# Low halves of sixteen weight panels and the decay masks on VectorE in place of GpSimd, in a two-layer streaming encoder on one core

## The chip, the cores and the metric

The kernel runs as one launch on one core of a Trainium2 chip. Its engines are named as in the profile: PE (TensorE, with PEld for its weight loads), DVE (VectorE), ACT (ScalarE), POOL (GpSimd) and SP (SyncE, whose queue starts most DMAs). The metric is the device time of the launch in microseconds (us); lower is better. Each engine takes its instructions in the order in which the program gives them, so an instruction that waits holds all that stand behind it on its engine.

## What is computed

One sequence of 1024 frames of width 1024 goes through two layers and a last RMSNorm. Layer 0 is chunked softmax attention, layer 1 a gated DeltaNet; each is followed by a squared-ReLU MLP. The change lies in layer 1. Cut to what matters there (chunks of 64 frames, 8 heads of width 128):

```
proj = h @ w_in                           # q, k, v, z of 8 heads each, and the gates a, b
qkv = silu(causal_conv(qkv, conv_w))      # 4 taps
gc = cumsum(g, axis=-1)                   # log decay inside a chunk
decay = exp(where(incl, gc[..., :, None] - gc[..., None, :], -inf))
L = where(strict, einsum('bhnid,bhnjd->bhnij', kb, k) * decay, 0.0)
M = L + eye(CHUNK)
sol = triangular_solve(M, rhs, left_side=True, lower=True, unit_diagonal=True)
qk = einsum('bhnid,bhnjd->bhnij', q, k) * decay
# scan over the 16 chunks:
v_new = u_c - w_c @ state
o_c = qd_c @ state + qk_c @ v_new
state = state * gl_c + kd_c^T @ v_new
```

## The kernel before

Every dense product is made from weight panels of 128 output columns, [128, 8, 128]. Matrices are split into a high and a low part, and each product is three matmuls: high by high, high by low, low by high. So a panel needs a `whi`, which ACT makes as a rounded copy of the loaded `wraw`, and a `wlo`, which is `wraw` less `whi`.

The delta layer (`deltanet`, L1673, to the end of `dn_run`) has 34 panels in the list `jobs` of `dn_ahead`: the keys of heads 0 to 7 (numbers 0 to 7), then q0, v0, q1, v1, q2, v2 (8 to 13), z0, q3 (14, 15), v3 and so on, and last two panels of the output projection. For each of the 32 others PE makes two halves of 512 frames, 24 matmuls each, into one of two PSUM banks (`acc`). The generator `weights` inside `dn_ahead` splits panel n in two pieces of 512 columns, high on ACT and low by `low` (L1015) on DVE or POOL. Panel 0 is split at the end of layer 0's MLP, the others inside `dn_run`.

A half that is done is taken out by `dn_evac` (L2076): DVE multiplies the bank into a tile `xp`, which frees the bank; ACT makes the first products of the convolution (`cy`, `cz`), DVE adds two taps, POOL adds `cy` and `cz`, ACT applies SiLU.

Beside these run the parts of the delta rule, each a generator with a priority:

- `dn_loads` (L2017) loads a row of log decays for each head into one of two tiles, `row` and `vT` in turn. The load for head h+2 waits until head h has used its tile.
- `dn_decays` (L2028) adds the causal mask to that tile in two pieces of 512 columns, then ACT makes eight exponentials of it.
- `dn_blocks` multiplies the key products by it, which gives the tile `U` of a head, and sends its diagonal blocks out. Four heads together are loaded back as `fu`.
- `dn_solves` inverts the 32x32 blocks of four heads by forward substitution, all on DVE: 31 steps, a product into `ft` and a sum into `fz`, of 1 to 961 elements per partition. It runs twice, first for heads 0 to 3, then for heads 4 to 7.
- `dn_scans` runs the scan of a head over 16 chunks: three fp32 matmuls a step on PE (`s<-st,WQ`, `s<-vn,kd`, `s<-vn,qk`) with two short DVE operations between them. Even and odd heads are two chains. The first needs the first forward substitution, the heads 4 to 7 need the second.
- `dn_outs` normalises and gates a head's output, `dn_reload` brings it back as the input of the output projection.

What order the engines see is decided while the program is written out. `Clock` holds a planned time for each engine; every instruction of this layer passes through `Engine.timed` (L160, call on L163, so nearly all of them carry the line L163) and adds its planned cost (`cost`, L106) to its engine. After each dense matmul `turn` gives each task a step when its planned time has come and, for priorities of 1 and more, when the planned backlog of DVE and ACT is below a limit. A DVE operation is planned at another cost than one on POOL, so the move of an operation between the two shifts what the planner puts beside what. The profile has the tile names of the program: `wlo<-wraw,whi` is a low part, `row<-row,mask` and `vT<-vT,mask` are the masks, `ft`, `fz` the forward substitution, `acc<-xs,whi` a dense matmul.

Of the kernel before, what the change touches and what calls it, by code (L numbers as in the profile page):

```python
# [207 lines left out]
class Trunk:  # L208
# [1554 lines left out]
    def dn_ahead(self):  # L1763

        H = 8
        self.jobs = jobs = [("k", n) for n in range(H)] + [(c, n) for n in range(3) for c in "qv"]
        for n in range(3, H):
            jobs += [("z", n - 3), ("q", n), ("v", n)]
        jobs += [("z", n) for n in range(5, H)]
        jobs += [("o", m) for m in range(2)]  # L1770
        raw, panel = {}, {}

        def fetch(n):
            if n < len(jobs):
                c, h = jobs[n]
                raw[n] = self.wp.tile([P, KT, P], F32, name=self.nm("wraw"), tag="wraw")
                self.nc.sync.dma_start(
                    raw[n], self.a["w_od"][h] if c == "o" else self.a["w_in"][8 * "qkvz".index(c) + h])

        def weights(n):  # L1780
            hi = self.wp.tile([P, KT, P], F32R, name=self.nm("whi"), tag="whi")
            lo = self.wp.tile([P, KT, P], F32R, name=self.nm("wlo"), tag="wlo")
            panel[n] = hi, lo
            for s in (slice(0, 4), slice(4, 8)):
                self.high(hi[:, s], raw[n][:, s])
                yield
                self.low(lo[:, s], raw[n][:, s], hi[:, s], True)
                yield
                yield
            fetch(n + 2)  # L1790

        def first():

            nc = self.nc
            ab = self.wp.tile([P, KT, P], F32, name=self.nm("wraw"), tag="wraw")
            nc.sync.dma_start(ab[:, :, 0:16], self.a["w_ab"])
            for _ in range(8):
                yield
            fetch(0)
            yield  # L1800
            yield
            self.wab = w = self.wp.tile([P, KT, P], F32R, name=self.nm("whi"), tag="whi")
            nc.gpsimd.memset(w[:, :, 16:32].bitcast(F32), 0.0)
            self.high(w[:, :, 0:16], ab[:, :, 0:16])
            yield
            self.low(w[:, :, 32:48], ab[:, :, 0:16], w[:, :, 0:16], True)
            yield
            fetch(1)
            yield from weights(0)

        self.panel, self.weights = panel, weights
        return first()
# [215 lines left out]
    def dn_decays(self, odd):  # L2028

        nc = self.nc  # L2030
        yield from self.until("rows")
        for h in range(odd, 8, 2):
            yield from self.until("load", h)
            if h < 2:
                yield from self.until("cols")
            d = self.heads.pop(("load", h))
            v = d.rearrange("p (q t) -> p q t", t=P)
            for q in range(2):
                u = v[:, 4 * q : 4 * q + 4]
                nc.gpsimd.tensor_tensor(  # L2040
                    u, u, self.mask.rearrange("p (o t) -> p o t", o=1).broadcast_to([P, 4, P]), ALU.add)
                yield
            for p in range(8):
                nc.scalar.activation(v[:, p], v[:, p], AF.Exp, bias=self.cols[:, 0, h, p : p + 1])
            yield
            for e in range(2):
                r = slice(64 * e, 64 * e + 64)
                nc.sync.dma_start(self.decay[h, r], v[r, :, r])
            yield
            self.heads["de", h] = d  # L2050
            self.mark("de", h)
            yield
# [614 lines left out]
```

## Time and profile before

| | before |
| --- | --- |
| time, median of 3 runs | 2569.77 us (2567.46 to 2570.54) |
| time of the profiled execution | 2571.22 us |
| its span | 2569.4 us |
| granted TensorE clock, mean | 0.988 |
| delta layer in the trace | about 1208 to 1838 us from the span's start |
| instructions | 36712 |

How to read it: a row of the grouped view gives the line, the engine, the operation, output and inputs, the shapes, the count, then the busy time in us with the mean of one in ns, then the idle time of the engine ahead of these instructions and what ended it. A row of the timeline gives the start in us, the duration, the instruction, its count and in brackets the idle time before it with its releaser. A row of the view of stretches gives the stretch, its length, then for PE, PEld, DVE, ACT and POOL busy time and instruction count, then the granted clock, the DMA share and GB/s.

### The profile page before, as it was taken

What the parts mean: (1) busy time and instruction counts of PE and PEld (TensorE: products, weight loads), DVE (VectorE), ACT (ScalarE), POOL (GpSimd) and SP (SyncE); (2) the same over time, 40 slices, a digit from 0 to 9 for tenths busy, and PEclk for the clock granted to TensorE, in tenths of its full rate; (3) what the DMA queues carried; (4) which work ended last, traced back from release to release, by engine and by line L of the source; (5) the groups of instructions that cost most, each with busy time, mean ns of one, the idle gap of its engine ahead of it and who ended that gap; (6) DMA issues with size and microseconds to landing.
All of it is one profiled execution on the core that took longest, in us unless ns stands there. A gap on an engine that the chain in (4) does not pass through costs nothing.

```text
span 2569.4 us, 36712 instructions
## 1 busy us (share of the span) xinstructions
PE 2466.1 (96%) x12638; PEld 2058.0 (80%) x12638; DVE 1901.5 (74%) x3299; ACT 1210.1 (47%) x2269; POOL 1293.5 (50%) x1088
## 2 busy tenths in 40 slices
PE   8999999999999999998888999999899999999997
PEld 6888888787888788886677788888787888787886
DVE  6665656678887788877578976676678788688887
ACT  6666567535555433334673333333335555433333
POOL 2444355514667466565474333332313766466655
PEclk9999999999999999999998999999999999999998
DMA  4222224424555977843343121122323555967752
GB/s 160 69 65 72 72 78 131 145 83 159 206 209 212 349 237 233 263 148 110 117 143 107 54 83 59 60 81 96 122 99 139 205 205 209 334 236 261 244 175 82
DMA packets 193082, 392.43 MB, mean 153 GB/s; under 512 B 54960, under 2 KB 61552, under 8 KB 192896
## 3 DMA queue, kind: packets, MB, share of 16 engines
q1 hardware_dynamic: 176048, 355.46, 41.3%
q10 hardware_dynamic: 16848, 34.63, 3.5%
q8 instruction: 100, 1.64, 0.3%
q14 instruction: 86, 0.70, 0.1%
HBM read 254.06 MB, written 127.57 MB: 149 GB/s over the span
## 4 chain that ended last, share of the span: by engine, by line
PE 60%; DVE 10%; DMA 5%; issue 3%; ACT 1%; POOL 1%; SPq 0%; ACTq 0%; DVEq 0%; POOLq 0%
PE y L1013 23%; PE z L1013 11%; PE acc L163 9%; PE acc L1013 6%; PE tp L163 4%; PE s L163 3%; PE acc L279 2%; PE acc L278 2%; PE acc L277 2%; DVE ft L163 2%; DMA xs<-gt 1%; DMA wraw<-in_w_down_dram 1%; DVE x L1517 1%; DMA wraw<-in_w_up_dram 1%; DVE wlo L1019 1%
## 5 line engine op out<-in xcount | busy, mean ns | idle before, releaser
L163 PE MATMUL acc<-xs,whi 128*128 128x512 f32 x1808 | 631.3, 412 | 10.0 <-DVE xp L163 6.1
L163 PEld LDWEIGHTS acc<-xs,whi 128*128 128x128 f32 x1808 | 333.3, 191 | 59.6 <-DVE xp L163 6.3
L163 PE MATMUL acc<-xs,wlo 128*128 128x512 f32 x896 | 368.4, 411 | 3.8 <-POOL wlo L163 3.8
L1013 PE MATMUL y<-xs,whi 128*128 128x512 f32 x1008 | 311.7, 390 | 5.2 <-DVE x L1517 1.8
L163 POOL TENSOR_TENSOR wlo<-wraw,whi 128x512 fp32r<-128x512 f32 x126 | 167.7, 1331 | 245.0 <-ACT whi L163 195.2
L1028 POOL TENSOR_TENSOR s<-wraw 128x256 f32<-128x256 f32 (+1 forms) x93 | 89.7, 965 | 353.9 <-DVE a L1019 175.1
L1019 DVE TENSOR_TENSOR wlo<-wraw,whi 128x512 fp32r<-128x512 f32 (+1 forms) x182 | 208.6, 1146 | 28.2 <-ACT whi L1022 28.2
L1013 PEld LDWEIGHTS y<-xs,whi 128*128 128x128 f32 x1008 | 188.9, 188 | 47.1 <-DVE x L1517 2.6
L1022 ACT ACTIVATE whi<-wraw 128x512 fp32r<-128x512 f32 (+2 forms) x191 | 146.5, 767 | 126.1 <-PE y L1013 87.3
L1013 PE MATMUL y<-xs,wlo 128*128 128x512 f32 x504 | 196.9, 391 | 7.0 <-DVE wlo L1019 6.8
L1013 PE MATMUL y<-xs,a 128*128 128x512 f32 x732 | 188.2, 392 | 9.1 <-DVE x L1517 9.1
L1022 ACT ACTIVATE a<-s 128x256 fp32r<-128x256 f32 x122 | 63.9, 525 | 282.2 <-PE y L1013 141.6
L163 PEld LDWEIGHTS acc<-xs,wlo 128*128 128x128 f32 x896 | 171.3, 191 | 29.2 <-POOL wlo L163 5.0
L1517 DVE TENSOR_TENSOR x<-y,x 128x512 f32<-128x512 f32 x240 | 165.1, 688 | 35.9 <-PE y L1013 28.8
L1013 PEld LDWEIGHTS y<-xs,a 128*128 128x128 f32 x732 | 135.9, 188 | 43.6 <-DVE x L1517 13.9
L1013 PE MATMUL acc<-xs,whi 128*128 128x512 f32 x528 | 162.8, 390 | 0.0
L1013 PE MATMUL y<-xs,ahi 128*128 128x512 f32 x512 | 158.7, 391 | 0.3 <-ACT nt L1206 0.3
L1095 DVE TENSOR_TENSOR c<-c 128x512 fp32r<-128x512 f32 x112 | 132.8, 1204 | 28.5 <-POOL c L1025 26.1
L163 POOL TENSOR_SCALAR pr<-pr,rs 128x640 f32<-128x640 f32 (+4 forms) x128 | 88.2, 692 | 129.2 <-DVE rs L163 98.1
L1013 PE MATMUL z<-xs,whi 128*128 128x512 f32 x480 | 147.8, 389 | 0.0
L163 POOL TENSOR_TENSOR cy<-cy,cz 128x512 f32<-128x512 f32 x48 | 69.0, 1438 | 147.1 <-DVE cz L163 125.2
L163 DVE CUSTOM_DVE_ANT_0 pr<-sp,bias 128x640 f32<-128x640 f32 (+4 forms) x128 | 83.8, 655 | 63.9 <-PE sp L163 62.9
(344 smaller groups left out, 6273.9 us busy)
## 6 DMA issues: line engine op xcount, KB each, us to landing
xs<-gt SPq DMA_DIRECT2D x256, 256.0 KB, 4.7
gt<-c SPq DMA_DIRECT2D x112, 512.0 KB, 2.9
wraw<-in_w_up_dram SPq DMA_DIRECT2D x64, 512.0 KB, 3.5
wraw<-in_w_down_dram SPq DMA_DIRECT2D x64, 512.0 KB, 4.5
r<-gr SPq DMA_DIRECT2D x88, 256.0 KB, 3.4
wraw<-in_w_in_dram SPq DMA_DIRECT2D x32, 512.0 KB, 3.4
gr<-ssum ACTq DMA_DIRECT2D x62, 256.0 KB, 3.2
wraw<-in_w_qkv_dram SPq DMA_DIRECT2D x30, 512.0 KB, 3.3
```

Source lines behind the costliest of these rows:

```text
L163: return call(*args, **more)
L277: nc.tensor.matmul(ps, hi[:, k], xh, start=(k == 0), stop=False)
L278: nc.tensor.matmul(ps, hi[:, k], xl, start=False, stop=False)
L279: nc.tensor.matmul(ps, lo[:, k], xh, start=False, stop=(k == KT - 1))
L1013: nc.tensor.matmul(ps, w[:, k], x, start=bool(first and f), stop=bool(last and e), skip_group_check=True)
L1019: self.nc.vector.tensor_tensor(lo, src, hi.bitcast(F32), ALU.subtract)
L1022: self.nc.scalar.activation(hi, src, AF.Copy)
L1028: self.nc.gpsimd.tensor_tensor(out, x, y, ALU.add)
L1095: nc.vector.tensor_tensor(t[z][:, HB:].bitcast(F32R), t[z][:, HB:], t[z][:, :HB], ALU.subtract)
L1517: nc.vector.tensor_tensor(x, ps, x, ALU.add)
```

## The change

The low parts of the panels 0 to 15 are made by DVE in place of POOL, two operations of 128x512 a panel. The sixteen mask additions (eight heads, two pieces of 128x512) are made by DVE as well. Nothing else is edited.

```
@@ -1784,7 +1784,7 @@
             for s in (slice(0, 4), slice(4, 8)):
                 self.high(hi[:, s], raw[n][:, s])
                 yield
-                self.low(lo[:, s], raw[n][:, s], hi[:, s], True)
+                self.low(lo[:, s], raw[n][:, s], hi[:, s], n >= 16)
                 yield
                 yield
             fetch(n + 2)
@@ -2037,7 +2037,7 @@
             for q in range(2):
                 u = v[:, 4 * q : 4 * q + 4]
-                nc.gpsimd.tensor_tensor(
+                nc.vector.tensor_tensor(
                     u, u, self.mask.rearrange("p (o t) -> p o t", o=1).broadcast_to([P, 4, P]), ALU.add)
                 yield
             for p in range(8):
```

So 32 low parts and 16 masks leave POOL for DVE. Because the planner prices them there, the order of the whole delta layer changes on every engine, from panel 1 on. Three places show it.

The first is DVE at the first two rows of decays (`row` is that of head 0, `vT` that of head 1; `gcols` ends the gates). Before, behind the copy into `gcols` the evacuations of the keys follow at once:

```order
L163 TENSOR_TENSOR xp_12549<-acc_12490,R_12294 128x512
L163 COPY gcols<-tp_12552 128x256
L163 SCALAR_TENSOR_TENSOR cy_12574<-xp_12549,convw,cy_12574 128x512
L163 SCALAR_TENSOR_TENSOR cz_12575<-xp_12549,convw,cz_12575 128x512
L163 MEMSET xp_12624 128x3
L163 TENSOR_TENSOR xp_12624<-acc_12567,R_12294 128x512
```

In the changed kernel two masks and a low part stand ahead of that work on the same engine:

```order
L163 TENSOR_TENSOR xp_12550<-acc_12490,R_12294 128x512
L163 COPY gcols<-tp_12553 128x256
L163 TENSOR_TENSOR row_12544<-row_12544,mask 128x512 x2
L163 TENSOR_TENSOR wlo_12569<-wraw_12390,whi_12568 128x512
L163 SCALAR_TENSOR_TENSOR cy_12578<-xp_12550,convw,cy_12578 128x512
L163 SCALAR_TENSOR_TENSOR cz_12579<-xp_12550,convw,cz_12579 128x512
L163 TENSOR_TENSOR vT_12562<-vT_12562,mask 128x512
L163 MEMSET xp_12618 128x3
L163 TENSOR_TENSOR xp_12618<-acc_12566,R_12294 128x512
```

The next evacuation of a bank (`xp_12624`, now `xp_12618`) has moved behind three masks and a low part. The masks wait for the loads of `row` and `vT`.

The second place is DVE in the first forward substitution, from its step of 100 elements on. Before, its steps follow each other:

```order
L163 TENSOR_TENSOR ft_13174<-fz_12321,fu_12320 128x100
L163 TENSOR_REDUCE fz_12321<-ft_13174 128x10
L163 TENSOR_TENSOR ft_13174<-fz_12321,fu_12320 128x121
L163 TENSOR_REDUCE fz_12321<-ft_13174 128x11
L163 TENSOR_TENSOR ft_13174<-fz_12321,fu_12320 128x144
L163 TENSOR_REDUCE fz_12321<-ft_13174 128x12
```

In the changed kernel low parts, masks and an evacuation stand between the same steps:

```order
L163 TENSOR_TENSOR ft_13266<-fz_12321,fu_12320 128x100
L163 TENSOR_REDUCE fz_12321<-ft_13266 128x10
L163 TENSOR_TENSOR wlo_13333<-wraw_13129,whi_13332 128x512
L163 TENSOR_TENSOR vT_13322<-vT_13322,mask 128x512
L163 TENSOR_TENSOR U_13356<-tp_13357,row_13169 128x512
L163 TENSOR_TENSOR ft_13266<-fz_12321,fu_12320 128x121
L163 TENSOR_REDUCE fz_12321<-ft_13266 128x11
L163 TENSOR_TENSOR vT_13322<-vT_13322,mask 128x512
L163 MEMSET xp_13387 128x3
L163 TENSOR_TENSOR xp_13387<-acc_13326,R_12294 128x512
L163 TENSOR_TENSOR wlo_13333<-wraw_13129,whi_13332 128x512
L163 TENSOR_TENSOR ft_13266<-fz_12321,fu_12320 128x144
```

Counted over the whole order of DVE: from the first instruction on `fu` (`frt<-fu`) to the end of the first substitution there stand 134 instructions before and 161 now, 12 of the new ones low parts, 4 masks, 4 `qk`, 2 `vb`, 2 `xp`, and few others. From there to the end of the second there are 194 and 190, 4 of these low parts. At the end of the first 22 halves have been evacuated before and 24 now, at the end of the second 32 and 34. Ahead of `frt<-fu` there are 12 in both, and there stand 14 low parts and 12 masks more than before.

The third place is PE near the end of the layer, in the scan of head 7 (`acc_17844` is its last half of a dense panel, `acc_17900` the output projection). From the tenth to the ninth last `s<-st,WQ` before:

```order
L163 MATMUL s_3782_17904<-st_17891,WQ_17613 128x128
L163 MATMUL acc_17844<-xs_11821,whi_17570 128x512 x2
L163 MATMUL acc_17844<-xs_11821,wlo_17571 128x512
L163 MATMUL acc_17844<-xs_11823,whi_17570 128x512
L163 MATMUL s_3783_17916<-vn_12244,kd_17498 128x128
L163 MATMUL s_3782_17904<-vn_12244,qk_12251 128x128
L163 MATMUL acc_17844<-xs_11823,whi_17570 128x512
L163 MATMUL acc_17844<-xs_11823,wlo_17571 128x512
L163 MATMUL acc_17844<-xs_11825,whi_17570 128x512
L163 MATMUL s_3785_17927<-st_17920,WQ_17613 128x128
```

In the changed kernel, from the tenth last to the eighth last:

```order
L163 MATMUL s_3787_17941<-st_17929,WQ_17626 128x128
L163 MATMUL s_3788_17949<-vn_12244,kd_17499 128x128
L163 MATMUL s_3787_17941<-vn_12244,qk_12251 128x128
L163 MATMUL s_3790_17956<-st_17953,WQ_17626 128x128
L163 MATMUL s_3791_17959<-vn_12245,kd_17499 128x128
L163 MATMUL s_3790_17956<-vn_12245,qk_12251 128x128
L163 MATMUL acc_17900<-xs_17837,whi_17738 128x512 x2
L163 MATMUL acc_17900<-xs_17837,wlo_17739 128x512
L163 MATMUL s_3793_17968<-st_17963,WQ_17626 128x128
```

The dense matmuls that lay between the scan's steps have been used up sooner. From the tenth last `s<-st,WQ` on 57 dense matmuls were left before, and 39 are left now.

More of the change, by code (lines that the diff above doesn't have):

```diff
@@ L1786, in weights @@
                 yield
-                self.low(lo[:, s], raw[n][:, s], hi[:, s], True)
+                self.low(lo[:, s], raw[n][:, s], hi[:, s], n >= 16)
                 yield
@@ L2039, in dn_decays @@
                 u = v[:, 4 * q : 4 * q + 4]
-                nc.gpsimd.tensor_tensor(
+                nc.vector.tensor_tensor(
                     u, u, self.mask.rearrange("p (o t) -> p o t", o=1).broadcast_to([P, 4, P]), ALU.add)
```

## The prediction

> **What bounds the kernel now.** The profile's page comes first. PE is busy nearly throughout, so the whole kernel is near PE's work; DVE has more to do than POOL.
>
> ```profile
> PE 2466.1 (96%) x12638; PEld 2058.0 (80%) x12638; DVE 1901.5 (74%) x3299; ACT 1210.1 (47%) x2269; POOL 1293.5 (50%) x1088
> ```
>
> That average says nothing of the layer that is edited, so the next view is that of stretches: the delta layer cut at the start and the end of the first forward substitution (1302 and 1391 us) and at the end of the second (1500).
>
> ```profile
> core 0: us, PE busy (x) PEld busy (x) DVE busy (x) ACT busy (x) POOL busy (x), PEclk, DMA share, GB/s
> 1208.00:1302.00 94.00, 82.92 (x394) 67.54 (x395) 48.70 (x102) 56.83 (x104) 48.96 (x41) 0.98 0.42 123
> 1302.00:1391.00 89.00, 71.51 (x325) 58.87 (x323) 86.08 (x135) 48.57 (x84) 52.27 (x36) 0.89 0.34 103
> 1391.00:1500.00 109.00, 102.24 (x755) 84.97 (x756) 98.05 (x201) 39.07 (x74) 40.47 (x34) 0.97 0.24 73
> 1500.00:1800.00 300.00, 293.08 (x2035) 257.91 (x2034) 198.77 (x511) 115.24 (x252) 97.69 (x73) 0.99 0.24 79
> ```
>
> DVE is half idle in the first stretch (45 us free), full in the second (86.08 of 89), nearly full in the third (98.05 of 109). From 1500 on PE is the bound (293 of 300). So a DVE operation is cheap before 1302, is paid in full from 1302 to 1391, and from 1500 on only PE's work counts. The waits say the same: of PE's waits from 1302 to 1392 the two longest end on DVE.
>
> ```profile
> PE tp L163 <- DVE vb L163: 6.1, 1, 6.1
> PE acc L163 <- DVE xp L163: 6.1, 1, 6.1
> ```
>
> Ahead of 1302 it is a low part from POOL that stops PE longest:
>
> ```profile
> PE acc L163 <- POOL wlo L163: 3.8, 2, 2.2
> ```
>
> **The change part by part.** 48 operations of 128x512 leave POOL: 32 low parts, 16 masks. Their rows there, and below them the same subtraction as DVE makes it elsewhere in this kernel:
>
> ```profile
> L163 POOL TENSOR_TENSOR wlo<-wraw,whi 128x512 fp32r<-128x512 f32 x126 | 167.7, 1331 | 245.0 <-ACT whi L163 195.2 <-DVE ru L300 26.3 <-PE acc L163 13.4
> L163 POOL TENSOR_TENSOR vT<-vT,mask 128x512 f32<-128x512 f32 x8 | 11.6, 1454 | 2.3 <-DMA vT<-grows 2.3
> L163 POOL TENSOR_TENSOR row<-row,mask 128x512 f32<-128x512 f32 x8 | 10.4, 1305 | 20.5 <-issue 8.6 <-DMA row<-grows 8.5 <-DVE ft L163 3.4
> L1019 DVE TENSOR_TENSOR wlo<-wraw,whi 128x512 fp32r<-128x512 f32 x120 | 121.5, 1013 | 5.0 <-ACT whi L1022 5.0
> L1019 DVE TENSOR_TENSOR wlo<-wraw,whi x182: 674/1176/2330, 554.4 to 2524.0; 128x512 fp32r<-128x512 f32 x120, 128x1024 fp32r<-128x1024 f32 x62
> ```
>
> So **the price** of one on DVE lies between 0.67 us (the shortest) and 1.01 us (the mean, beside a busy POOL). I take 0.82, the middle, since POOL keeps the `cy` and `cz` sums there. No row shows a mask on DVE; it has the same shape and two SBUF inputs, so it gets the same price.
>
> **What a removed POOL operation gives back** is in the timelines of DVE and POOL at the start of the substitution:
>
> ```profile
> 1303.88 0.19 DVE L163 SCALAR_TENSOR_TENSOR ru<-ru,frt 128x32 f32<-128x32 f32 x1
> 1304.10 1.32 DVE L163 SCALAR_TENSOR_TENSOR ru<-ru 128x32 f32<-128x32 f32 x1
> 1305.45 1.22 DVE L163 SCALAR_TENSOR_TENSOR ry<-ru,ry 128x32 f32<-128x32 f32 x1
> 1306.70 1.20 DVE L163 TENSOR_TENSOR ru<-ry 128x32 f32<-128x32 f32 x1
> 1307.94 1.19 DVE L163 SCALAR_TENSOR_TENSOR ru<-ru,frt 128x32 f32<-128x32 f32 x1
> ```
>
> ```profile
> 1304.10 1.27 POOL L163 TENSOR_TENSOR wlo<-wraw,whi 128x512 fp32r<-128x512 f32 x1 [1.44 <-DVE ru L163]
> 1305.34 1.29 POOL L163 TENSOR_TENSOR vT<-vT,mask 128x512 f32<-128x512 f32 x1
> 1306.58 1.28 POOL L163 TENSOR_TENSOR cy<-cy,cz 128x512 f32<-128x512 f32 x1
> 1307.82 1.27 POOL L163 TENSOR_TENSOR cz<-cy,cz 128x512 f32<-128x512 f32 x1
> ```
>
> The same DVE operation takes 0.19 us alone and 1.19 beside a POOL operation: each POOL operation here takes 1.0 us from DVE. That is the upper bound of what one gives back; the lower is 0, where DVE sits idle or reads PSUM. The sum of `ft` bounds it in the whole: the same 31 products in the first substitution and, with POOL less busy, in the second.
>
> ```profile
> L163 DVE TENSOR_TENSOR ft<-fz,fu 128x1 f32<-128x1 f32 (+30 forms) x31 | 32.8, 1057 | 0.5
> ```
>
> ```profile
> L163 DVE TENSOR_TENSOR ft<-fz,fu 128x1 f32<-128x1 f32 (+30 forms) x31 | 27.6, 891 | 0.3
> ```
>
> I take half, 0.5 us. The Trainium skill, "SBUF — State Buffer", section "SBUF: two separate sides", says that VectorE with two SBUF inputs and a GpSimd operation that reads SBUF exclude each other over one port pair for a whole instruction, the loser waiting in full. The four rows above agree. By that rule the moved operations, which have two SBUF inputs, are blocked by the sums that stay on POOL, and block them; that speaks against the change and is the third rival.
>
> Now the terms, in order.
>
> (a) Ahead of 1302 (14 low parts, 12 masks more): 26 x 0.82 = 21 us of DVE, into 45 us of idle time. The cover is there. The path through this stretch is load, mask, exponentials, `U`, the next load. A mask pair falls from 2 x 1.3 to 2 x 0.68, over two rounds about -2.5 us, and PE's 3.8 us for low parts go in part. Against it stands the queue: DVE now waits itself where POOL waited for the load.
>
> ```profile
> 1247.33 1.27 POOL L163 TENSOR_TENSOR row<-row,mask 128x512 f32<-128x512 f32 x1 [7.15 <-DMA row<-grows]
> ```
>
> ```profile
> 1241.58 0.69 DVE L163 TENSOR_TENSOR xp<-acc,R 128x512 f32<-128x512 f32 x1 [0.18 <-PE acc L163]
> 1255.04 1.50 DVE L163 SCALAR_TENSOR_TENSOR cy<-xp,convw,cy 128x512 f32<-128x512 f32 x1 [12.77 <-ACT cy L163]
> ```
>
> Behind the first mask pair now stand a low part, `cy`, `cz` and the evacuation that ran at 1241.58; but DVE stood idle for 12.77 us there anyway. I take -2 us, bounds -6 to +8 (second rival). On SP the loads keep their order behind the stores of `U`.
>
> (b) First substitution, 1302 to 1391, DVE full: 16 moved operations x 0.82 = +13.1. The new order puts other work in as well (two `xp`, a `cy`, two `vb`, less one `U`, each of the shape of the `xp` above and so about 0.7; four `qk` at 0.42; three small ones, 0.3 in all): 2.8 + 1.7 + 0.3 = +4.8. In that stretch 11 low parts and 6 masks leave POOL, 17 x 0.5 = -8.5. Sum +9.4.
>
> ```profile
> L163 DVE TENSOR_TENSOR qk<-tp,dc 64x256 f32<-64x256 f32 x12 | 5.0, 420 | 4.3 <-PE tp L163 4.2
> ```
>
> (c) Second substitution: 4 x 0.82 = +3.3, less 4 x 0.5, less the `qk`, `vb`, `st` that have moved ahead (3.6): -2.3. It ends at -2 + 9.4 - 2.3 = +5.1 us.
>
> (d) By then two halves more are evacuated, 48 dense matmuls. In a full stretch three of them take 0.68 us, so 48 are 10.9 us of PE's work, and PE is the bound from here on: -10.9.
>
> ```profile
> 1318.00 0.39 PE L163 MATMUL acc<-xs,wlo 128*128 128x512 f32 x1
> ...
> 1318.68 0.39 PE L163 MATMUL acc<-xs,wlo 128*128 128x512 f32 x1
> ```
>
> (e) The end of the scan. With nothing dense between, a step takes 2.1 us:
>
> ```profile
> 1809.62 0.38 PE L163 MATMUL s<-st,WQ 128*128 128x128 f32 x2
> ...
> 1819.70 0.46 PE L163 MATMUL s<-st,WQ 128*128 128x128 f32 x2 [0.31 <-ACT o L163]
> ...
> 1821.86 0.49 PE L163 MATMUL s<-st,WQ 128*128 128x128 f32 x2 [0.34 <-DVE st L163]
> ...
> 1837.89 0.39 PE L277 MATMUL acc<-xs,whi 128*128 128x512 f32 x1
> ```
>
> From the tenth last `s<-st,WQ` to the output projection's L277 it took 28.3 us with 57 dense matmuls inside; ten bare steps are 21 us. With 39 inside it is 25.4 us if half of those still hide, 28.3 at most, while 18 (4.1 us) have moved ahead of it. So +1.2 to +4.1; I take +3.
>
> Sum: 5.1 - 10.9 + 3 = **-2.8 us**. The profiled execution took 2571.22 us (span 2569.4), 1.5 above the median of 2569.77; taken from the median this gives 2567.0. A measurement of this kernel can tell about 0.2%, 5.1 us, from no change: the forecast is no change, with a lean to faster.
>
> **The rivals.** First, **faster**: POOL's blocking goes nearly whole (1.0 us each, as in the four rows) and the operations cost 0.68. Then (b) is 10.9 + 4.8 - 17 = -1.3 in place of +9.4, the sum -13.5, the time about 2556. For it: the evacuation for which PE waited 6.1 us stood behind sixteen bare steps and now stands among them. Against it: `ft` lost only 5.2 us more in the first substitution than in the second.
>
> Second, **slower**, by the queue on DVE: the mask pair of head 2 waits for its load with `U` of head 1 behind it, and the load of head 3 waits for that `U`. Before, POOL waited there 8.6 us (the "issue" in the row of `row` masks), and nobody else did. If DVE stands for all of that, the load of head 3, its exponentials, `U` and `fu` come up to 8 us later, and (a) is +8: 2577. It decides from about 5 us of waiting on. For it: the order has that `U` between the two masks. Against it: the load of head 3 queued behind that of head 2 before as well.
>
> Third, **slower**, by the ports: each moved operation takes 1.01 us, as DVE's low parts do elsewhere, and nothing comes back since the remaining sums now hit a denser DVE. (b) gains 3 + 8.5: about 2578.5.
>
> **How the numbers follow.** Forecast 0.40 (own range 2564.6 to 2574.9), first rival 0.33, second 0.17, third 0.10. The range takes in the rivals, 2556 and 2578.5, with the bounds of (e) and the runs' own scatter: 2555 to 2581. Faster by over 0.2%: 0.34; within: 0.39; slower: 0.27.
>
> **What would show it.** POOL has 48 operations fewer and DVE 48 more. In the stretch from `frt` to the last `fz` DVE stays full and is 5 to 12 us longer, while PE's busy time in it rises and its wait for `xp` shrinks; `ft` x31 falls below 32.8 us. `fu` lands about when it did. The second substitution ends some 5 us later, with two halves more done. If `frt` starts over 5 us later with DVE waiting for `row<-grows`, the second rival holds; if the low parts on DVE average 1 us or more, the third; if the first substitution takes no longer than 89 us, the first. A new wait of PE for scan steps around 1500 to 1800 would break (d), which takes PE as the bound there.

## The result and the profile after

The changed kernel takes 2596.14 us in the median (2593.6 to 2597.95, 4 runs) where the kernel before, on the same chip, takes 2570.15 us (2567.46 to 2572.34, 4 runs). The ratio is 1.0095, with a 95% interval of 1.0084 to 1.0107: about **26 us slower**. The forecast was 2567.0 and the range ended at 2581, so the prediction was wrong in sign and in size. The profiled execution took 2597.69 us (span 2595.8), with a mean granted clock of 0.983 (0.988 before).

First, where in the program the time was lost. These are the same four stretches of the view of stretches as before, in the changed kernel (length, then busy time of PE, PEld, DVE, ACT, POOL, then granted clock, DMA share, GB/s):

```profile
1208.00:1302.00 94.00, 83.59 (x398) 68.82 (x397) 55.06 (x124) 56.94 (x106) 21.34 (x20) 0.96 0.45 118
1302.00:1391.00 89.00, 82.75 (x379) 68.83 (x378) 79.80 (x153) 47.02 (x84) 29.14 (x20) 0.90 0.38 108
1391.00:1500.00 109.00, 100.25 (x728) 82.83 (x727) 98.64 (x197) 37.02 (x70) 34.19 (x29) 0.95 0.26 74
1500.00:1800.00 300.00, 280.87 (x1886) 243.31 (x1884) 207.98 (x493) 109.34 (x238) 89.83 (x66) 0.96 0.21 67
```

POOL is emptier in all of them, as intended (21.34 for 48.96 in the first). The row that matters is the last: PE, the bound there before with 293.08 of 300 at a clock of 0.99, now has 280.87 at 0.96, with fewer instructions done.

Second, DVE's waits ahead of 1302 (engine and tile, what it waited for, us in total, times, longest), and the masks' own row:

```profile
DVE row L163 <- DMA row<-grows: 16.7, 3, 6.3
DVE vT L163 <- DMA vT<-grows: 6.6, 1, 6.6
```

```profile
L163 DVE TENSOR_TENSOR wlo<-wraw,whi 128x512 fp32r<-128x512 f32 x30 | 22.6, 756 | 3.8 <-ACT whi L163 3.7
L163 DVE TENSOR_TENSOR vT<-vT,mask 128x512 f32<-128x512 f32 x8 | 6.4, 799 | 13.2 <-DMA vT<-grows 13.2
L163 DVE TENSOR_TENSOR row<-row,mask 128x512 f32<-128x512 f32 x8 | 6.2, 784 | 16.7 <-DMA row<-grows 16.7
```

The moved operations are cheap, 0.76 to 0.80 us each. What is dear is the last column: DVE stands 29.9 us in front of masks whose rows have not landed, and all that is queued behind them stands too.

Third, PE's waits from 1509, the end of the second forward substitution, to the end of the layer:

```profile
PE s L163 <- DVE vn L163: 14.0, 18, 2.2
PE s L163 <- DVE ry L163: 4.5, 3, 2.4
PE s L163 <- DVE st L163: 3.2, 2, 2.6
```

PE now stops 21.7 us for single steps of the scan. In the kernel before, from the end of its second substitution on, the three longest such rows come to 10.8 us:

```profile
PE s L163 <- DVE vn L163: 6.9, 7, 2.1
PE s L163 <- DVE rt L163: 2.9, 1, 2.9
PE s L163 <- DVE xp L163: 1.0, 1, 1.0
```

The milestones of all profiled executions, in us from the span's start, from the timelines: `frt<-fu` (start of the first substitution), the start of its last `fz`, the first `s<-st,WQ` (first scan step), the first L277 (end of the layer), and the last less the third. Each row is from one execution, so a difference of 2 us says nothing.

| kernel | frt | last fz | first scan step | L277 | scan |
| --- | --- | --- | --- | --- | --- |
| before | 1302.1 | 1389.0 | 1428.4 | 1837.9 | 409.5 |
| changed | 1312.5 | 1405.2 | 1450.0 | 1865.7 | 415.7 |
| e1_masks | 1309.7 | 1405.0 | 1450.4 | 1864.6 | 414.2 |
| e2_lows | 1304.0 | 1405.2 | 1450.8 | 1854.0 | 403.2 |
| e3_old_order | 1308.4 | 1399.2 | 1438.5 | 1848.7 | 410.2 |
| e4_new_order | 1313.7 | 1406.1 | 1450.0 | 1863.1 | 413.1 |
| e5_fewer | 1303.5 | 1390.0 | 1428.9 | 1827.6 | 398.7 |
| e6_late | 1309.6 | 1400.5 | 1443.0 | 1852.0 | 409.0 |
| e7_lows_old | 1299.0 | 1383.5 | 1423.2 | 1833.7 | 410.5 |
| e8_front | 1299.2 | 1385.6 | 1424.5 | 1835.7 | 411.2 |
| e9_more | 1307.8 | 1400.4 | 1444.7 | 1863.2 | 418.5 |
| e10_solve5 | 1298.4 | 1382.7 | 1427.0 | 1842.3 | 415.3 |
| e11_solve7 | 1297.7 | 1383.4 | 1424.5 | 1841.7 | 417.2 |
| e12_masks_old | 1303.9 | 1395.4 | 1433.3 | 1841.2 | 407.9 |

The layer is 629.6 us long before (from 1208.3, the start of the gates) and 655.9 after (from 1209.8): the loss lies in it. The scan starts 21.6 us later, and then takes 6.2 us longer than it did, though 97 dense matmuls fewer are left for it (from the first scan step to L277 PE starts 963 before and 866 now). Two questions follow: what makes the scan start later, and why it isn't shorter.

### The profile page after: what moved, and what is told of

It reads as the page before. It is cut to its first block, busy times and chain, and to the rows that moved or that the text cites. A ratio compares the mean times of both kernels' runs of the same rounds, so it can differ in the third digit from the quotient of the medians.

```text
span 2595.8 us, 36691 instructions
## 1 busy us (share of the span) xinstructions
PE 2487.7 (96%) x12638; PEld 2070.3 (80%) x12638; DVE 1931.1 (74%) x3347; ACT 1206.4 (46%) x2267; POOL 1230.7 (47%) x1040
## 4 chain that ended last, share of the span: by engine, by line
PE 56%; DVE 12%; DMA 5%; issue 3%; ACT 3%; POOL 1%; SPq 1%; ACTq 0%; DVEq 0%; POOLq 0%
PE y L1013 23%; PE z L1013 11%; PE acc L163 6%; PE acc L1013 6%; PE tp L163 3%; PE s L163 3%; PE acc L279 1%; PE acc L277 1%; PE acc L278 1%; DVE ft L163 1%; DMA wraw<-in_w_up_dram 1%; DMA xs<-gt 1%; DMA row<-grows 1%; DVE x L1517 1%; DVE cz L163 1%
## 5 line engine op out<-in xcount | busy, mean ns | idle before, releaser
L163 POOL TENSOR_TENSOR wlo<-wraw,whi 128x512 fp32r<-128x512 f32 x96 | 126.6, 1318 | 256.8 <-ACT whi L163 214.9
L163 ACT ACTIVATE o<-s 64x128 f32<-64x128 f32 x128 | 34.8, 272 | 211.7 <-PE s L163 199.0
```

The source lines that it names most:

```text
L163: return call(*args, **more)
```

## The experiments

**First four: which part, and engine or order?** The change does two things at once. It sends 48 instructions to another engine, and it makes the planner charge another price, which shifts the order of everything. The two can be parted: charge the planner for one engine and issue on the other.

e1_masks, the kernel before with the masks alone:

```diff
-                nc.gpsimd.tensor_tensor(
+                nc.vector.tensor_tensor(
```

> Masks alone on DVE, low parts on POOL as before. The change took the kernel from 2570 to 2596 us; the first forward substitution started 10.4 us later and DVE waited some 32 us for the row loads in front of masks. Theory Q (the queue on DVE: a mask that waits for its load holds U and the evacuations behind it): nearly the whole loss is here, 2588 to 2597, with frt about 10 us late and DVE waiting over 15 us for row and vT. Theory P (the price of the moved low parts in the full substitution, 16 x 0.7 to 1.0): little, 2570 to 2576. Theory O (the planner's new order, in which the first inverse stands 85 to 90 dense matmuls later on PE, whatever engine the operations run on): this order is shifted as much as that of the whole change, so 2588 to 2597 too, but without need of a wait on DVE.

e2_lows, the low parts alone:

```diff
-                self.low(lo[:, s], raw[n][:, s], hi[:, s], True)
+                self.low(lo[:, s], raw[n][:, s], hi[:, s], n >= 16)
```

> Low parts of panels 0 to 15 alone on DVE, masks on POOL as before. Theory Q: no mask is on DVE, so frt starts within 3 us of where it did and the time is 2566 to 2574. Theory P: the loss of the substitution is here, 6 to 10 us, 2576 to 2581. Theory O: the first inverse stands 90 dense matmuls later here as well, so 2586 to 2596.

e3_old_order, both on DVE with the planner charged for POOL (`planned("gpsimd", "vector")`), and e4_new_order, both on POOL with the planner charged for DVE (`planned("vector", "gpsimd")`). Both use this in place of the calls in `weights` (for the panels below 16) and in `dn_decays`:

```diff
+    def planned(self, plan, run):
+        nc = self.nc
+        if not isinstance(nc, Metered):
+            return getattr(nc, run).tensor_tensor
+        def go(out, x, y, op):
+            self.clock.spend(plan, "tensor_tensor", (out, x, y, op), {})
+            return getattr(nc.real, run).tensor_tensor(out, x, y, op)
+        return go
```

> Both moved to DVE, but the order on PE, ACT and in the program is that of before: the planner is charged for POOL, the instruction goes to DVE. Theory Q: the masks stand where POOL waited for their loads, so DVE waits there too: frt 5 to 12 us late, 2578 to 2590. Theory P: 2576 to 2581, frt on time. Theory O: the order is the old one, so 2567 to 2575.

> The order on PE and ACT of the changed kernel, but low parts and masks run on POOL as before (the planner is charged for DVE). Theory Q: no mask waits on DVE, 2568 to 2575. Theory P: the same, 2567 to 2573. Theory O: the order alone costs, 2585 to 2596, and PE waits for scan steps between 1500 and 1850 us as in the changed kernel (vn over 12 us).

Measured against 2569.8 us of the kernel before in these runs:

| run | us | ratio, 95% interval |
| --- | --- | --- |
| e1_masks | 2596.47 | 1.0101 (1.0086 to 1.0116) |
| e2_lows | 2585.55 | 1.0060 (1.0044 to 1.0077) |
| e3_old_order | 2578.29 | 1.0032 (1.0019 to 1.0044) |
| e4_new_order | 2598.65 | 1.0106 (1.0091 to 1.0121) |

**The order alone costs all of it**: in e4 nothing runs on another engine than before, and it is 29 us slower. The engines alone, in the old order, cost 8.5 us. They don't add up (37 against 26), so in the new order the engines cost nothing more. Each half of the change shifts the order by itself, and is slow by itself: e1 and e2 both have the first scan step at 1450, as the whole change has. e2, at 2585.55, lies just under the range that was expected of the order.

How the order delays `frt` is seen on DVE ahead of the first substitution, in the timeline of the changed kernel (start, duration, instruction, in brackets the wait ahead of it):

```profile
1294.95 0.69 DVE L163 TENSOR_TENSOR row<-row,mask 128x512 f32<-128x512 f32 x1 [4.71 <-DMA row<-grows]
1295.56 0.68 DVE L163 TENSOR_TENSOR U<-tp,vT 128x512 f32<-128x512 f32 x1
...
1298.63 0.68 DVE L163 TENSOR_TENSOR U<-tp,vT 128x512 f32<-128x512 f32 x1
...
1309.41 0.69 DVE L163 TENSOR_TENSOR vT<-vT,mask 128x512 f32<-128x512 f32 x1 [6.07 <-DMA vT<-grows]
...
1312.48 0.18 DVE L163 TENSOR_SCALAR frt<-fu 128x32 f32<-128x32 f32 x1
```

The new order puts a mask of head 4 ahead of `U` of head 3, and DVE stands 4.71 us in front of it for its row. The load of `fu` needs this `U`. It starts 5.7 us later than before and takes longer to land, 6.3 us for 3.5. The loads of the kernel before and of the changed one, and their time to landing:

```profile
1298.56 0.34 SPq L2199 DMA_DIRECT2D fu<-ud  x1
fu<-ud SPq DMA_DIRECT2D x1, 512.0 KB, 3.5
```

```profile
1304.26 0.34 SPq L2199 DMA_DIRECT2D fu<-ud  x1
fu<-ud SPq DMA_DIRECT2D x1, 512.0 KB, 6.3
```

So `fu` is there at 1302.1 before and at 1310.6 now. A mask of head 5 stands ahead of `frt` as well, and `frt`, which belongs to heads 0 to 3, has no use for it. But it can have cost no more than the 1.9 us from 1310.6 to 1312.5. In e4 the mask of head 4 waits on POOL, and reaches `U` of head 3 by a detour. POOL, then DVE, of e4:

```profile
1290.69 1.29 POOL L1023 TENSOR_TENSOR row<-row,mask 128x512 f32<-128x512 f32 x1 [4.21 <-DMA row<-grows]
1291.95 1.28 POOL L163 TENSOR_TENSOR cy<-cy,cz 128x512 f32<-128x512 f32 x1
1293.19 1.30 POOL L163 TENSOR_TENSOR cz<-cy,cz 128x512 f32<-128x512 f32 x1
```

```profile
1294.52 1.76 DVE L163 SCALAR_TENSOR_TENSOR cz<-xp,convw,cz 128x512 f32<-128x512 f32 x1 [8.21 <-POOL cz L163]
...
1296.82 0.68 DVE L163 TENSOR_TENSOR U<-tp,vT 128x512 f32<-128x512 f32 x1
```

The mask holds POOL, the sum into `cz` stands behind it, DVE waits 8.21 us for that sum, and the second piece of `U` stands behind that. The mask of head 5 does the same to `frt`, which starts 4 us after `fu` has landed. So whichever engine takes the masks, `frt` comes 10 to 12 us late.

Yet the scan starts as late without a late `frt`: in e2 `frt` is only 1.9 us late, and the first substitution still ends at 1405 and the first scan step still comes at 1450.8, as in the whole change.

**Next four: the place in the order, the bound in the scan, and the low parts by themselves.** In PE's order the first scan step stands 97 dense matmuls later in the changed kernel. e6_late puts it 81 later by a longer pause ahead of the substitutions, with all engines as before; what the planner then places elsewhere moves with it. e5_fewer takes away 64 dense matmuls in the scan of the kernel before without a change of order (the planner is still charged). e7_lows_old and e8_front move low parts alone in the old order.

```diff
-'sl_solve': 9.0
+'sl_solve': 18.0
```

> Engines of before; the planner's pause ahead of each forward substitution is 18 us in place of 9, which puts the end of the first substitution 82 dense matmuls later in the order and the end of the second 54 later, just where the order of the changed kernel has them; nothing else is edited. Theory S (the place of the substitution in the order sets when the scan starts, and the layer ends some 410 us after that): 15 to 28 us slower, 2585 to 2598, with the first scan step at about 1450. Theory Q' (the changed order costs by its front, where masks, U and loads stand behind other work, not by the place of the substitution): below 2578.

```diff
+                        if 16 <= n < 32 and m == 2 and k in (2, 5):
+                            self.clock.spend("tensor", "matmul", (ps, w[:, k], x), {})
+                        else:
                             nc.tensor.matmul(ps, w[:, k], x, start=(k == m == 0), stop=(k == KT - 1 and m == 2))
```

> Engines and order of before; 64 of the 768 dense matmuls of the panels 16 to 31 (two of the eight low-by-high products in each half) are left out, so the output lacks those products. They lie in the scan after the second substitution, as the 66 do that the changed kernel has used up by then. Theory B (PE is the bound from 1500 on, as the prediction's term d took it): 64 x 0.227 = 14.5 us less, 2555 to 2558. Theory F (the dense matmuls are the filler of the scan: without them PE waits for scan steps, and each hole is followed by a stretch at half clock): at most a third of it comes back, 2564 to 2575, PE's waits for vn and st in 1495 to 1840 grow over 20 us and the granted clock there falls below 0.98.

```diff
-                self.low(lo[:, s], raw[n][:, s], hi[:, s], True)
+                if n < 16:
+                    self.planned("gpsimd", "vector")(lo[:, s], raw[n][:, s], hi[:, s].bitcast(F32), ALU.subtract)
+                else:
+                    self.low(lo[:, s], raw[n][:, s], hi[:, s], True)
```

e8_front has `1 <= n < 7` as its condition, so the panels 1 to 6.

> Order of before, low parts of panels 0 to 15 on DVE, masks left on POOL (the planner is charged for POOL throughout). With both moved in this order it was +8.5 us, frt 6.3 us late and the substitution 3.9 us longer. Theory Q (masks that wait for their rows hold DVE): without them frt is on time and the time is 2570 to 2575. Theory P (the low parts' price and the shared port carry it): still 2576 to 2580.

> Order of before, low parts of panels 1 to 6 alone on DVE (12 operations, all ahead of the first substitution, where DVE was half idle), everything else on POOL. If DVE's idle time there covers them and PE's wait of 3.8 us for low parts goes: 2564 to 2570. If they hold up U and the evacuations on DVE: frt later by 2 to 5 us and 2572 to 2576.

Measured against 2570.1 us:

| run | us | ratio, 95% interval |
| --- | --- | --- |
| e5_fewer | 2560.19 | 0.9958 (0.9944 to 0.9973) |
| e6_late | 2586.27 | 1.0060 (1.0038 to 1.0082) |
| e7_lows_old | 2568.94 | 0.9991 (0.9979 to 1.0002) |
| e8_front | 2567.80 | 0.9989 (0.9979 to 0.9998) |

e6: 16.2 us slower from a later place of the substitutions, with the first scan step 14.6 us later (1443.0; 1450 was expected) and the layer's end 14.1 later. e2, whose first scan step is as late as that of the whole change, is 15.8 us slower. That is over half of what the whole order costs. The rest, 10 to 13 us, is there in the kernels in which the masks have DVE's price (e1, e4 and the changed one), and it lies behind the first scan step: from there to L277 they take 413 to 416 us, e2 403.2. What in their order makes it, no run here shows.

e5: 9.9 of the 14.5 us came back, between the two theories and nearer to the first, and the granted clock stayed at 0.99. **In the order of before PE is, for the most part, the bound in the scan**, as the prediction had read it.

e7 and e8: in the old order the low parts cost nothing on DVE. `frt` even starts 3 us earlier and PE's wait of 3.8 us for `POOL wlo` is gone from the list of its waits. Over the runs it is a gain of 0.1%, which e7's interval doesn't part from nothing and e8's hardly does.

**Last four: filler in the new order, the place moved the other way, and the masks by themselves.** e9_more adds 64 dense matmuls to the scan of the changed kernel, where e5 took 64 from that of before:

```diff
+                        if 16 <= n < 32 and m == 2 and k in (2, 5):
+                            nc.real.tensor.matmul(ps, w[:, k], x, start=False, stop=False)
```

> The changed kernel with 64 dense matmuls more: two of the low-by-high products in each half of the panels 16 to 31 are issued twice, so the output holds them twice. They lie in the scan after the second substitution, about as many as the changed order lacks there against before. The changed kernel itself is at 2596. Theory B (PE is the bound in that stretch): 64 x 0.227 = 14.5 us more, 2609 to 2612. Theory F (they fill holes in which PE waits for scan steps, and the half-clock stretches of 3.4 us behind these holes go): at most 7 us more, 2594 to 2603, PE's waits after 1509 fall and the granted clock there rises over 0.96.

e10_solve5 and e11_solve7 are e7 with `'sl_solve'` at 5.0 and 7.0. e12_masks_old has the masks alone through `planned("gpsimd", "vector")`.

> The kernel with low parts 0 to 15 on DVE in the old order (2569), with the planner's pause ahead of each forward substitution 5 us in place of 9: the end of the first substitution stands some 13 dense matmuls earlier in the order, that of the second 37 earlier. Theory S (the layer ends some 410 us after the scan starts, and the scan starts as the place of the substitution in the order allows): the first scan step 3 to 8 us before 1423 and 2561 to 2567. Rival: fu lands no earlier, DVE waits for it with everything behind it, and nothing is gained or it is 2 to 8 us slower, 2569 to 2577.

> As the run with 5 us, with a pause of 7 us: the ends of the substitutions stand 14 and 21 dense matmuls earlier. Theory S: 2562 to 2568. Rival (DVE waits for fu): 2569 to 2575.

> Order of before, masks alone on DVE (the planner is charged for POOL), low parts on POOL. Both moved in this order was +8.5, the low parts alone -1.2. Theory Q (a mask that waits for its row holds what stands behind it on DVE): +8 to +11, 2578 to 2581, frt 5 to 7 us later than 1302, DVE's waits for row and vT over 12 us. If the two act only together (the low parts make DVE full, then the masks hurt): below 2574.

Measured against 2571.61 us:

| run | us | ratio, 95% interval |
| --- | --- | --- |
| e9_more | 2599.38 | 1.0104 (1.0088 to 1.0120) |
| e10_solve5 | 2574.62 | 1.0013 (1.0003 to 1.0022) |
| e11_solve7 | 2572.65 | 1.0005 (0.9997 to 1.0014) |
| e12_masks_old | 2578.03 | 1.0024 (1.0012 to 1.0036) |

e9: **64 matmuls more cost the changed kernel next to nothing** (1.0104 beside 1.0095, 2 us, with intervals that overlap), where 64 fewer gained the old one 9.9. The stretch from the end of the second substitution to the end of the layer, in the changed kernel and in e9:

```profile
1509.00:1866.00 357.00, 333.06 (x2168) 287.14 (x2169) 238.73 (x586) 131.33 (x288) 106.25 (x78) 0.95 0.23 76
```

```profile
1502.00:1863.00 361.00, 339.39 (x2221) 292.04 (x2222) 237.70 (x585) 131.68 (x289) 106.01 (x78) 0.97 0.23 76
```

In these two executions they filled holes, stretches in which PE waits (its idle time falls from 23.9 to 21.6 us) and the granted clock rose from 0.95 to 0.97. The rise of the clock is not shown over the runs: the profiled execution of e9 is its fastest, 6.4 us under its median, and the mean clock of the whole program is 0.983 to 0.986 in its four executions, 0.982 to 0.987 in those of the changed kernel. The time is clear of the 14.5 us that 64 matmuls would add. In the new order, then, PE is not the bound in the scan; it waits for scan steps that have too little dense work beside them.

e10 and e11: theory S falls in this direction. The first substitution ends hardly earlier (1382.7 and 1383.4 against 1383.5 of e7), the first scan step doesn't come earlier (1427.0 and 1424.5 against 1423.2) and the time is the same or 0.1% worse. As the rival had it, DVE now waits in front of `frt` for the load of `fu`, 8.8 us in e10 and 5.1 in e11. A later place costs, an earlier one brings nothing.

e12: 6.4 us slower, less than the 8 to 11 expected, in an order in which the low parts cost nothing. So most of the engines' 8.5 us of e3 are those of the masks. DVE's waits in e12, ahead of 1302 and behind it:

```profile
DVE row L1023 <- issue: 12.9, 2, 8.7
DVE row L1023 <- DMA row<-grows: 6.5, 1, 6.5
...
DVE vT L1023 <- DMA vT<-grows: 4.8, 2, 4.2
```

```profile
DVE vT L1023 <- DMA vT<-grows: 5.3, 2, 3.6
DVE row L1023 <- DMA row<-grows: 5.2, 1, 5.2
```

The "issue" of 8.6 us that POOL had ahead of a mask before has come to DVE, with the waits for the loads. `frt` was only 1.8 us late in this execution (5 to 7 were expected): most of the loss is inside the first substitution, 91.5 us for 86.9, where masks wait 10.5 us.

Apart from e5, which leaves products out, no kernel here is clearly better than the one before; e8, at 0.9989, is the nearest to it.

## Why the prediction was wrong

**Price of a moved operation**: 0.82 predicted, 0.76 measured for the low parts, 0.78 and 0.80 for the masks. Right, and the rival that put it at 1.01 is out.

**(a), ahead of the substitution**: -2 with bounds of -6 and +8; measured +10.4 (1302.1 to 1312.5, of which 1.5 lie ahead of the layer), outside the bounds. The step that failed is "DVE stood idle for 12.77 us there anyway". It took the first pair of masks for all of them. Behind the first pair there was indeed idle time; the later ones wait 4.7 to 6.6 us each in the trace of after, among live work. This is the mechanism of the second rival, which had +8 and a chance of 0.17, with `fu` late as it said and not "about when it did". Only the place is another. Behind the mask of head 2 the second piece of `U` of head 1 does come 8.3 us later (1272.67 for 1264.40), but by the load for head 4 that is made up: it goes out 0.4 us later than before. What holds `fu` is the mask of head 4 ahead of `U` of head 3, and e4 shows that it does not need DVE for it.

**(b), first substitution**: +9.4 predicted, +5.8 measured (86.9 to 92.7 us). The give-back came about as taken; the same 31 products, in the changed kernel, for 32.8 before:

```profile
L163 DVE TENSOR_TENSOR ft<-fz,fu 128x1 f32<-128x1 f32 (+30 forms) x31 | 25.6, 827 | 0.3
```

That is 7.2 us less on `ft` alone, where 8.5 was taken for the whole stretch. PE's busy time there rose, as said. With low parts alone in the old order (e7) the substitution takes 84.5 us, less than before: the first rival had that part right.

**(c), second substitution**: -2.3 predicted, -2.7 measured (106.5 to 103.8 us between the two last `fz`).

**(d) is the step that decided**: -10.9 predicted, and -7.9 together with (e). From the second substitution's end to the layer's, the stretch of both, it took 342.4 us before (1495.5 to 1837.9) and takes 356.7 now (1509.0 to 1865.7), **+14.3**. The layer's end came 27.8 us later in these executions where the sum had -2.8, and 22 of the 31 us between them lie here. The prediction saw that two halves more, 48 dense matmuls, would be done by then, and took them off PE's work, since PE is the bound there. That reading of the old profile was right for the most part (e5). It doesn't carry over to the new order, since dense matmuls are not only PE's work in the scan but also its cover: they fill the time between a scan step on PE and its answer from DVE. The same count of the order, 24 halves in place of 22 at the end of the first substitution, says that the substitution stands later among the dense matmuls. It was booked as work done ahead; it is a scan that starts later with less beside it. e6, which makes most of that shift with the engines as before, is 16 us slower. The sign that the prediction named for a broken (d), a new wait of PE for scan steps, is there: 14.0 us in 18 waits for `vn`, 6.9 in 7 before.

Where the time went can be counted on PE. Ahead of the first scan step PE lost nothing: from the start of the gates that stretch is 20.1 us longer (240.2 for 220.1), and it holds 97 dense matmuls more, 22.0 us of work at 0.227. From the first scan step to L277 these 97 are missing, 22.0 us less of PE's work. PE's idle time there rises from 15.9 to 27.1 us (409.5 less 393.6 busy, 415.7 less 388.6), +11.2. The time lost to a clock below full, the sum of one less the granted clock over stretches of 1 us, rises from 3.4 to 18.7 us, +15.3. Together +4.5, of the +6.2 that was measured; the rest stays unassigned. In the whole layer 18.8 us are lost to the clock before and 34.1 after.

How the loss is shared between idle time and clock differs from execution to execution. The profiled one had a mean clock of 0.983 over the program, which is 44 us lost (31 before). Another of the four had 0.987, some 34 us lost, and still took 2593.6 us. So the slow clock by itself is not what the loss comes down to. It is one form in which the missing cover shows, in the profiled execution more than half of it.

One hole in PE's work, at the end of the second substitution, in the timelines of PE and DVE:

```profile
1507.48 0.39 PE L163 MATMUL s<-vn,qk 128*128 128x128 f32 x2
1507.62 0.47 PE L163 MATMUL acc<-xs,wlo 128*128 128x512 f32 x1
1510.70 0.46 PE L163 MATMUL s<-st,WQ 128*128 128x128 f32 x2 [2.60 <-DVE st L163]
...
1514.38 0.63 PE L163 MATMUL acc<-xs,wlo 128*128 128x512 f32 x1
...
1518.30 0.39 PE L163 MATMUL acc<-xs,wlo 128*128 128x512 f32 x1
```

```profile
1507.13 1.84 DVE L163 TENSOR_TENSOR ft<-fz,fu 128x961 f32<-128x961 f32 x1
1509.01 1.16 DVE L163 TENSOR_REDUCE fz<-ft 128x31 f32<-128x961 f32 x1
1510.20 0.35 DVE L163 SCALAR_TENSOR_TENSOR st<-st,gl,s 128x128 f32<-128x128 f32 x1
```

One dense matmul stands between two scan steps. DVE has the largest product of the substitution ahead of `st`, 3 us of it, and PE waits 2.60. Then a dense matmul takes 0.63 us where it took 0.39, for almost seven microseconds: the clock has halved, which the stretches of 2 us show (clock in the third column from the right):

```profile
1508.00:1510.00 2.00, 0.10 (x1) 0.00 (x0) 1.97 (x2) 0.81 (x2) 1.09 (x1) 1.00 0.00 0
1510.00:1512.00 2.00, 0.93 (x4) 0.77 (x5) 0.80 (x3) 1.80 (x2) 0.17 (x1) 0.76 0.51 211
1512.00:1514.00 2.00, 1.90 (x8) 1.50 (x8) 1.64 (x4) 1.48 (x4) 0.34 (x1) 0.50 0.59 244
1514.00:1516.00 2.00, 2.00 (x9) 1.54 (x7) 1.41 (x3) 0.62 (x2) 0.94 (x1) 0.50 0.24 82
1516.00:1518.00 2.00, 2.00 (x9) 1.81 (x8) 0.55 (x2) 0.54 (x2) 0.00 (x0) 0.53 0.87 276
1518.00:1520.00 2.00, 2.00 (x13) 1.70 (x12) 0.57 (x2) 0.00 (x0) 0.00 (x0) 1.00 0.05 7
```

So a wait of 2.6 us cost 6 (2.6 and half of 6.8). The prediction's price for a wait was its length.

**(e), the end of the scan**: +3 predicted, with bounds of 1.2 and 4.1; from the tenth last `s<-st,WQ` to L277 it took 28.3 us before and takes 30.8 now (1834.9 to 1865.7), where the prediction allowed 28.3 at most; with the 4.1 us that have moved ahead this is +6.6. Two half-clock stretches, at 1838 and 1849, were not in it: 5.1 us are lost to the clock here, 1.7 before.

What stays open: why the order of the whole change costs 10 to 13 us more than a later place of the substitutions (e1, e4 and the changed kernel against e2 and e6); and what the holes would cost at a full clock, since no run here kept the holes and changed only the clock.

## What to carry to other kernels

Where a planner writes the order, a changed engine is a changed price, and the new order can be the larger part of the change, as here: run the new order on the old engines and the old order on the new engines before anything is said of either engine. Moving independent work ahead of a latency-bound chain is a gain only as far as the chain keeps cover; count what is left beside it, not what is done before it. An instruction that waits for a load blocks its whole queue, and queues that feed each other, so look for whom it holds and not for the idle time of the engine it joins.

## What the hardware showed that was not expected

TensorE's clock drops to 0.50 in pieces. In nearly all of the low stretches of these traces the time lost is 1.7 us or a multiple of it, that is some 3.4 us at half clock at a time: 11 such pieces in the layer before, 20 after. The Trainium skill, "TensorE: Matmul & The Clock Gate", section "Part 1: The HAM clock gate (the "warmup" mystery)", says that the clock is either full or half and that it halves after an idle window of about 3.4 us. The trace agrees with the two levels and with the length. It differs on the idle time that it takes: the hole above is 2.60 us long, and one of 1.84 us, at 1559.8, was also followed by 3.4 us at half clock:

```profile
1561.63 0.49 PE L163 MATMUL s<-vn,kd 128*128 128x128 f32 x2 [1.84 <-DVE vn L163]
```

By that rule no wait of PE in the changed kernel's scan, the longest 2.6 us, would have cost more than itself.

A longer hole can go free. In the kernel before, PE's longest wait in the scan, 2.86 us, was followed by full clock:

```profile
1778.39 0.46 PE L163 MATMUL s<-st,WQ 128*128 128x128 f32 x2 [2.86 <-DVE rt L163]
```

```profile
1778.00:1780.00 2.00, 1.61 (x8) 1.43 (x9) 1.82 (x9) 0.00 (x0) 0.00 (x0) 1.00 0.43 141
1780.00:1782.00 2.00, 2.00 (x13) 1.75 (x13) 1.30 (x7) 0.27 (x1) 0.36 (x1) 1.00 0.31 125
```

The traces suggest why. All half-clock pieces of an execution's layer begin whole multiples of 3.413 us apart; in the changed kernel those at 1511.06, 1538.36 and 1562.26 are 8 and 7 such steps apart. On this grid the holes of 2.60 and 1.84 us each lie inside one step, and the next step is at half clock. The hole of 2.86 us is cut by a boundary into 1.25 and 1.61 us. So what a hole costs seems to depend on where it falls on the grid as well. That would let executions of one kernel differ in the clock, as the four here do (0.982 to 0.987).
